# Weight differences moved from GpSimd to VectorE, norms by half rows, and last rows finished as two halves, in a one-core decoder block

## The chip, the cores and the metric

The kernel runs on one core of one Trainium2 chip. A core has TensorE (PE, matrix multiply), VectorE (DVE), ScalarE (ACT), GpSimd (POOL) and SyncE (SP, which here only issues DMAs); DMA engines move data between device memory and the on-chip SBUF, and TensorE writes to PSUM banks. The metric is the device time of one execution in microseconds (us); less is better. Line numbers, as L1287, are lines of the kernel before.

## The reference

One decoder block on a residual stream of 1024 tokens by 1024 columns, all in float32: RMS norm, 8 heads of forgetting attention and 8 heads of stick-breaking attention, an output projection onto the residual; RMS norm and cross-attention over 256 memory tokens (4 heads); RMS norm and a gated feed-forward with a causal convolution of width 3 over 2 x 2816 columns; a last RMS norm. Cut to the parts that the change touches:

```python
o = jnp.einsum('bhqk,bhkd->bhqd', p.astype(v.dtype), v)
x = x + jnp.einsum('bsc,cd->bsd', _merge(o), w_o)      # memory output, onto the residual
h = _rmsnorm(x, ffn_norm_g[l])                         # feed-forward norm
u = jnp.einsum('bsd,df->bsf', h, w_up[l])
...
x = x + jnp.einsum('bsf,fd->bsd', jax.nn.silu(gate) * val, w_down[l])
return _rmsnorm(x, final_norm_g)                       # last norm
```

`_rmsnorm` multiplies each row by the inverse root of the mean of its squares plus 1e-6, and by a gain.

## The kernel before

**Float32 as pairs.** A float32 operand is split into a high part (rounded by ScalarE or GpSimd) and a low part (the rest, subtracted by VectorE); `mm3` (L208 to L210) makes a product of three matmuls, high by high, high by low and low by high. So each operand costs a rounding and a subtraction, and TensorE waits for the later of the two.

**Fast products.** The memory output, the up product and the down product use a seven-product scheme for 2 x 2 blocks: sums and differences of operand blocks are formed first, and the products are added to several outputs. The residual x lies in eight tiles of 128 rows, `xr[0]` to `xr[7]`, each of two half rows of 512 columns (`lo_`, `hi_`).

**The planned stretch.** From the memory values to the first two of 22 up blocks the order is not written out but planned: `on(engine, length, function, after, take, give, at, ...)` adds a step with an assumed length, the steps it follows, the buffers it takes and gives, and a due time `at`, and `Plan.run` lays the steps out by simulating the engines. Among the steps that are ready on an engine the one with the smallest `at` goes first, and none starts more than 12 (`AHEAD`) before its `at`. What comes out is an order for each engine's queue; the times are forgotten. On the chip each queue is then worked off strictly in that order, so that a step that waits holds up all behind it. SyncE's queue (loads and spills) and GpSimd's (sums, splits, small powers, and the DMAs that add to their destination) are ordered this way too.

**Steps around the change, in order of their due times.** `values_steps` makes the memory values of the second half of the tokens; `mo_steps(k, ...)` makes product 7, 5, 3, 6 and 4 of the memory output (`o7`, `o5`, `o3`, `o6`, `o4`), each of four steps f of two splits (ACT high, L1308, DVE low, L1311) and four matmul groups of three. `outs` adds the banks of a product to `xr` or to a helper (`u`, L1344); `accumulate` adds a helper to `xr[4 + j]` by a DMA that GpSimd issues (L1144). The weight differences `t2s` (b11 = b22 - b11, VectorE) and `t4s` (b21 = b21 - b11, GpSimd), both at L1287, feed o6 and o4:

```python
t2s = [on(DVE, LOW, tt(V, b11[f], b22[f], b11[f], sub), [split_steps[5, 1][f]], at=58 + f, lock=True) for f in range(4)]
t4s = [on(POOL, SUM, tt(G, b21[f], b21[f], b11[f], sub), [loads[6 + f // 2], t2s[f]], at=66 + f, lock=True)
       for f in range(4)]
```

`finals[row]` collects what must be done before a row of x is complete. `norm_steps(0, 78)` and `norm_steps(1, 85)` then make the feed-forward norm of rows 0 to 3 and 4 to 7: a square of the whole row with its sum (ACT, L1427), mean (DVE, L1430), inverse root as a power (POOL, L1434), scaling into a tile `xn` (DVE, L1437), and a spill of the row to device memory (`spills`, SP). `tr` transposes the four scaled rows on TensorE (L1450), and the transposes are split into operands `b` (L1467, L1471) and, in the second half, `t1` and `t2` with sums formed by DMAs onto `f` (`onto_f1`). There are seven `xn` buffers. `gate_steps` and `sum_steps` make the weight operands of the first up blocks: four sums on GpSimd for each (L1611) and splits (L1595 to L1600). The up products read all of these.

**The loop and the end.** The 20 other up blocks run in a plain loop, then the down product (`dn_product`) in seven passes of eleven steps. The last passes complete rows 4 to 7 and rows 0 to 3: `finish` adds the bank to the low half of the row (L1956), squares both halves (L1961), adds the two sums (L1962), takes mean and power (L172, L174), multiplies the whole row by the root and the gain (L1964), and stores it (L1965).

Of the kernel before, what the change touches and what calls it, by code (L numbers as in the profile page):

```python
# [10 lines left out]
F32 = mybir.dt.float32  # L11
# [125 lines left out]
def hybrid_block(ctx, tc, x, mem, w, wf, pcol, bfg, fing, out):  # L137
# [1194 lines left out]
    finals = {j: [] for j in range(TB)}  # L1332
# [23 lines left out]
    for j in range(4):  # L1356
        def copy(j=j):
            A.activation(a22n12[j], o5[j], AF.Copy)

        c_ = on(ACT, ROUND, copy, [split_steps[5, "out"][j]] + [accs["s4x", i] for i in range(2)], at=outs_at)  # L1360
        outs(5, j, "STPS"[j], ([j], add_to(xr[j][:, hi_], o5, j)), after=[c_])
        finals[4 + j].append(accumulate(("p5", j), xr[4 + j][:, hi_], a22n12[j], [c_], 58))
# [6 lines left out]
    t4s = [on(POOL, SUM, tt(G, b21[f], b21[f], b11[f], sub), [loads[6 + f // 2], t2s[f]], at=66 + f, lock=True)  # L1369
# [4 lines left out]
    for j in range(4):  # L1374
        outs(3, j, "PSPS"[j], ([j], add_to(xr[j][:, hi_], o3, j, sub, True)))
# [3 lines left out]
    for j in range(4):  # L1379
        l_ = outs(6, j, "PSPS"[j], ([j], add_to(xr[j][:, hi_], o6, j)), ([], add_to(u[j], o6, j)), after=[u7[j]])  # L1380
        for c in (hi_, lo_):
            finals[4 + j].append(accumulate(("v", j, c.start), xr[4 + j][:, c], u[j], l_, 76))
# [32 lines left out]

    ssr = [[small.tile([P, 4], F32, tag=g, bufs=2, name=g) for g in ("ss", "rs")] for _ in range(2)]
    xns, spills = {}, {}

    def norm_steps(th, at):
        out_ = []  # L1420
        ss, rs = ssr[th]
        for j in range(4):
            row = 4 * th + j

            def square(j=j, row=row):
                xns[th, j] = wk.tile([P, D], F32, tag="xn", name="xn")
# [27 lines left out]
    norm0 = norm_steps(0, 78)  # L1454
# [180 lines left out]
    sum_steps(0, g0, v0, 86, {"m": [tmps], "s1": free, "s2": free, "s3": free, "a22": free, "s4": []}, {"s4": ["xn"]})  # L1635


    norm1 = norm_steps(1, 85)
    t_steps = {}

    def rest(i):

        if "rest" not in tiles:
            t = [qkp["f"].tile([P, 1024], F32R, tag=g, name=f"bt_{g}", bufs=b) for g, b in
                 (("q", 2), ("q", 2), ("k1", 2), ("k1", 2), ("k20", 1))]
            t = sum([views(t_, 2) for t_ in t], [])
            for n in range(3):
                t += views(vp.tile([P, 2, 1024], F32R, tag="v", name=f"bt_v{n}").rearrange("p k c -> p (k c)"), 4)
            tiles["rest"] = t
        return tiles["rest"][i]  # L1650
# [42 lines left out]
    for k in range(4):  # L1693
# [14 lines left out]
        x_ = last_turn = on(PE, 436, turn, norm1, ["T"], ["xn"] * 4 * (k == 3), at=86 + k)  # L1708
# [167 lines left out]
    def dn_product(fa, fb, held=0, done=None):  # L1876
# [10 lines left out]
        for f in range(H):  # L1887
# [169 lines left out]
```

## Time and profile before

| | us |
|---|---|
| median of 3 runs (lowest, highest) | 1600.13 (1599.53, 1602.65) |
| profiled execution, its own time | 1604.29 |
| span from first to last instruction in it | 1602.2 |
| busy in the span: PE, DVE, ACT | 1529.2, 1214.4, 783.8 |
| busy in the span: POOL | 533.3 |
| granted TensorE clock, share of full speed | 0.989 |

TensorE is busy for 95% of the span, so its idle stretches are what can be won; an average over the span does not say where they are. Busy time of an engine counts an instruction from its start to its end, also where it is held up inside.

### The profile page before, as it was taken

To read this page: it belongs to the slowest core of one execution; us is meant where nothing else is said; L and a number is where in the kernel's file an instruction comes from. 1 tells how busy PE (TensorE), PEld (TensorE's weight loads), DVE (VectorE), ACT (ScalarE), POOL (GpSimd) and SP (SyncE) were. 2 spreads that over 40 slices of the span, in tenths; PEclk is the share of its full clock that TensorE was granted. 3 is DMA by queue.
4 is the path that set the end of the run, shared out by engine and by line. 5 is a ranking of instruction groups with operands and counts; after the bars stand their busy time and mean duration, and the time that the engine had idled before them with its cause. 6 is when DMAs were issued, how large, how long until landed. Compare 5 with 4: busy or idle time off the path is not lost.

```text
span 1602.2 us, 22089 instructions
## 1 busy us (share of the span) xinstructions
PE 1529.2 (95%) x7684; PEld 1270.6 (79%) x7684; DVE 1214.4 (76%) x2070; ACT 783.8 (49%) x1534; POOL 533.3 (33%) x652
## 2 busy tenths in 40 slices
PE   7999999999999888999999889999999999999997
PEld 7677887887898766878887767878888888788886
DVE  7378777877877774365439988999999999786565
ACT  7368768757867551043325463333333333444443
POOL 3032323432432210123222445544445442233331
PEclk9999999999999999999999999999999999999998
DMA  5211021111115557312146454222222223998782
GB/s 178 95 66 66 27 64 60 37 54 66 40 54 184 193 164 247 122 53 78 42 141 161 92 145 139 76 83 93 86 85 79 79 82 107 325 291 198 146 180 105
DMA packets 78223, 183.54 MB, mean 115 GB/s; under 512 B 8728, under 2 KB 8856, under 8 KB 77856
## 3 DMA queue, kind: packets, MB, share of 16 engines
q1 hardware_dynamic: 62976, 152.63, 27.6%
q0 software_dynamic: 14688, 29.37, 10.3%
q8 instruction: 60, 0.98, 0.3%
q14 instruction: 51, 0.42, 0.1%
q10 hardware_dynamic: 448, 0.14, 0.0%
HBM read 130.69 MB, written 33.59 MB: 103 GB/s over the span
## 4 chain that ended last, share of the span: by engine, by line
PE 61%; DVE 17%; issue 8%; ACT 6%; DMA 5%; POOL 2%; SPq 0%; POOLq 0%; DVEq 0%; ACTq 0%
PE up_p L208 4%; PE up_p L209 4%; PE up_p L210 4%; PE dn L209 4%; PE dn L210 4%; PE dn L208 4%; PE pt L746 3%; PE pq L208 2%; PE pq L209 2%; PE pq L210 2%; PE po L763 2%; PE pqm L210 2%; PE pqm L209 2%; PE pqm L208 2%; PE po L762 2%
## 5 line engine op out<-in xcount | busy, mean ns | idle before, releaser
L703 POOL TENSOR_TENSOR p<-p,aw 128x383 f32<-128x383 f32 (+4 forms) x64 | 79.7, 1245 | 175.4 <-DVE aw L697 144.6
L209 PE MATMUL dn<-opb,opa 128*128 128x512 f32 x308 | 120.8, 392 | 2.7 <-DVE opb L1529 2.7
L754 DVE TENSOR_TENSOR ptl<-pt,pth 128x512 fp32r<-128x512 f32 x192 | 103.5, 548 | 25.2 <-ACT pth L750 23.7
L750 ACT ACTIVATE pth<-pt 128x512 fp32r<-128x512 f32 x192 | 92.7, 490 | 61.1 <-PE pt L746 55.2
L210 PE MATMUL dn<-opb,opa 128*128 128x512 f32 x308 | 120.8, 392 | 0.0
L208 PE MATMUL dn<-opb,opa 128*128 128x512 f32 x308 | 118.7, 390 | 0.7 <-ACT opb L1526 0.7
L746 PE MATMUL pt<-zid,p 128*128 128x128 f32 x576 | 95.3, 274 | 4.7 <-DVE ptl L754 4.5
L746 PEld LDWEIGHTS pt<-zid,p 128*128 128x128 f32 x576 | 72.4, 141 | 23.8 <-DVE ptl L754 6.9
L1540 POOL TENSOR_TENSOR tmp<-wv 128x512 f32<-128x512 f32 x20 | 33.4, 1672 | 166.0 <-DMA wv<-in_w_dram 156.1
L412 DVE TENSOR_TENSOR wlo<-wraw,whi 128x512 fp32r<-128x512 f32 x84 | 69.4, 854 | 20.7 <-ACT whi L407 20.3
L763 PE MATMUL po<-ptl,v 128*128 128x512 f32 x192 | 69.0, 359 | 9.6 <-DVE ptl L754 9.4
L1770 ACT ACTIVATE yv<-cv,cw 128x1024 f32<-128x1024 f32 x22 | 27.4, 1243 | 99.3 <-DVE cv L1802 98.7
L194 POOL TENSOR_SCALAR whi<-wraw 128x512 fp32r<-128x512 f32 x48 | 30.2, 643 | 134.7 <-issue 51.7
L680 POOL TENSOR_SCALAR p<-p,fx 128x128 f32<-128x128 f32 (+3 forms) x64 | 49.0, 768 | 74.9 <-DVE fx L620 64.2
L209 PE MATMUL up_p<-b,a 128*128 128x512 f32 x176 | 68.7, 390 | 1.9 <-DVE b L1471 1.9
L209 PEld LDWEIGHTS dn<-opb,opa 128*128 128x128 f32 x308 | 58.3, 189 | 15.2 <-DVE opb L1529 3.1
L208 PE MATMUL up_p<-b,a 128*128 128x512 f32 x176 | 68.8, 391 | 1.0 <-ACT b L1467 1.0
L762 PE MATMUL po<-pth,v 128*128 128x512 f32 x192 | 68.6, 357 | 0.7 <-ACT pth L750 0.6
L210 PE MATMUL up_p<-b,a 128*128 128x512 f32 x176 | 68.5, 389 | 0.0
L208 PEld LDWEIGHTS dn<-opb,opa 128*128 128x128 f32 x308 | 57.9, 188 | 13.2 <-ACT opb L1526 1.1
L210 PEld LDWEIGHTS dn<-opb,opa 128*128 128x128 f32 x308 | 58.3, 189 | 12.3
L407 ACT ACTIVATE whi<-wraw 128x512 fp32r<-128x512 f32 x84 | 50.0, 626 | 30.9 <-DMA wraw<-in_w_dram 16.1
(502 smaller groups left out, 5225.7 us busy)
## 6 DMA issues: line engine op xcount, KB each, us to landing
wraw<-in_w_dram SPq DMA_DIRECT2D x136, 256.0 KB, 3.0
a_d<-yv SPq DMA_DIRECT2D x22, 512.0 KB, 2.6
wg<-in_w_dram SPq DMA_DIRECT2D x20, 512.0 KB, 3.4
wv<-in_w_dram SPq DMA_DIRECT2D x20, 512.0 KB, 3.5
dn<-a_d POOLq DMA_DIRECT2D x32, 256.0 KB, 7.1
dn<-a_d SPq DMA_DIRECT2D x24, 256.0 KB, 8.7
dn<-in_w_dram SPq DMA_DIRECT2D x24, 256.0 KB, 7.8
xr<-mos POOLq DMA_DIRECT2D x20, 256.0 KB, 5.5
```

The source lines that it names most:

```text
L208: T.matmul(o, lt[0], rt[0], start=start, stop=False)
L209: T.matmul(o, lt[0], rt[1], start=False, stop=False)
L210: T.matmul(o, lt[1], rt[0], start=False, stop=stop)
L407: A.activation(t["hi"][:, c], t["raw", n], AF.Copy)
L412: in_turn("low", lambda: V.tensor_tensor(t["lo"][:, c], t["raw", n], t["hi"][:, c].bitcast(F32), op=ALU.subtract))
L680: G.tensor_scalar(out=c_["p"], in0=c_["p"], scalar1=c_["fx"][:, 4:5], scalar2=0.0, op0=ALU.mult, op1=ALU.add)
L703: G.tensor_tensor(c_["p"][:, :n0 - 1], c_["p"][:, :n0 - 1], c_["a"][:, 1:], op=ALU.mult)
L746: T.transpose(pt[:, j * P:(j + 1) * P], self.rows[j]["p"][:, kb * P:(kb + 1) * P], ident)
L750: A.activation(t[:, 512 - n:], self.sp["pt", kb][:, 512 - n:], AF.Copy)
L754: V.tensor_tensor(t[:, 512 - n:], self.sp["pt", kb][:, 512 - n:], self.sp["th", kb][:, 512 - n:].bitcast(F32), op=ALU.subtract)
L762: T.matmul(self.po[:, c], lv, self.sp["th", kb][:, c], start=kb == 0, stop=False)
L763: T.matmul(self.po[:, c], lv, self.sp["tl", kb][:, c], start=False, stop=kb == 4 * self.g + 3)
```

## The change

Seven edits, in the order of the diff:

1. `finals` is kept for each half row; the halves of a row become complete separately.
2. The four differences `t4s` go from GpSimd to VectorE, due at 58 + f in place of 66 + f. The DMAs that add `u` to rows 4 to 7 are due at 74 in place of 76.
3. The feed-forward norm squares a row as two half rows, each once its half is complete, into the weight tile `b22` as scratch, with the factor 1/1024 inside the square; the mean is one instruction that adds the two sums and the epsilon. The norm of rows 0 to 3 is due at 70 in place of 78 (and its low-half squares 8 earlier than that step's others), that of rows 4 to 7 at 85.5 in place of 85.
4. The scaled rows 6 and 7 lie in a tile of another pool (`xnv` in `vp`); the first half's norm takes its `xn` buffer at the scaling and not at the square.
5. `sum_steps` of the first up block is due at 95 in place of 86.
6. The tiles that the second half's operands lie in are allocated one by one at first use.
7. In `finish` the high half of each row, complete before the last product, is squared and multiplied by the gain (on GpSimd) ahead, in `half_done`; after the product the low half alone is added, squared and multiplied by root and gain (VectorE) while ScalarE multiplies the high half by the root. `half_done` of the last four rows is called before the last matmuls of the last pass.

The diff, cut where lines only move or repeat:

```diff
-    finals = {j: [] for j in range(TB)}
+    finals = {(j, c): [] for j in range(TB) for c in range(2)}
...
-    t4s = [on(POOL, SUM, tt(G, b21[f], b21[f], b11[f], sub), [loads[6 + f // 2], t2s[f]], at=66 + f, lock=True)
+    t4s = [on(DVE, LOW, tt(V, b21[f], b21[f], b11[f], sub), [loads[6 + f // 2], t2s[f]], at=58 + f, lock=True)
            for f in range(4)]
...
-        for c in (hi_, lo_):
-            finals[4 + j].append(accumulate(("v", j, c.start), xr[4 + j][:, c], u[j], l_, 76))
+        for n, c in ((1, hi_), (0, lo_)):
+            finals[4 + j, n].append(accumulate(("v", j, c.start), xr[4 + j][:, c], u[j], l_, 74))
...
+    free_b22 = split_steps[3, 1] + t2s
+
+    def xn_tile(th, j):
+
+        if th and j > 1:
+            return lazy("xv", lambda: vp.tile([P, 2, D], F32, tag="v", name="xnv"))[:, j - 2, :]
+        return wk.tile([P, D], F32, tag="xn", name="xn")
...
-            def square(j=j, row=row):
-                xns[th, j] = wk.tile([P, D], F32, tag="xn", name="xn")
-                A.activation(xns[th, j], xr[row], AF.Square, accum_out=ss[:, j:j + 1])
+            def square(c, j=j, row=row):
+                A.activation(b22[j], xr[row][:, (lo_, hi_)[c]], AF.Square, scale=D ** -0.5, accum_out=(ss, rs)[c][:, j:j + 1])
 
             def mean(j=j):
-                V.tensor_scalar(out=rs[:, j:j + 1], in0=ss[:, j:j + 1], scalar1=1.0 / D, scalar2=EPS,
-                                op0=ALU.mult, op1=ALU.add)
+                V.tensor_scalar(out=ss[:, j:j + 1], in0=ss[:, j:j + 1], scalar1=rs[:, j:j + 1], scalar2=EPS,
+                                op0=add, op1=add)
...
             def scale(j=j, row=row):
+                xns[th, j] = xn_tile(th, j)
                 V.tensor_scalar(out=xns[th, j], in0=xr[row], scalar1=rs[:, j:j + 1], scalar2=None, op0=ALU.mult)
 
-            q_ = on(ACT, 1060, square, finals[row], ["xn"], at=at + j)
-            q_ = on(DVE, 150, mean, [q_], at=at + j)
+            e_ = 1 - th
+            sq = [on(ACT, ROUND + 200, lambda c=c, f=square: f(c), finals[row, c] + free_b22, at=at + j + ((-10, -2), (-2, -2))[th][c])
+                  for c in (th, 1 - th)]
+            q_ = on(DVE, 150, mean, sq, at=at + j + -2.5)
             q_ = on(POOL, 550, power, [q_], at=at + j - 3)
-            out_.append(on(DVE, 760, scale, [q_], at=at + j))
+            out_.append(on(DVE, 760, scale, [q_], ["xn"] * (not th or j < 2), at=at + j))
...
-    norm0 = norm_steps(0, 78)
+    norm0 = norm_steps(0, 70)
...
-    sum_steps(0, g0, v0, 86, {"m": [tmps], "s1": free, "s2": free, "s3": free, "a22": free, "s4": []}, {"s4": ["xn"]})
+    sum_steps(0, g0, v0, 95.0, {"m": [tmps], "s1": free, "s2": free, "s3": free, "a22": free, "s4": []}, {"s4": ["xn"]})
-    norm1 = norm_steps(1, 85)
+    norm1 = norm_steps(1, 85.5)
...
-        x_ = last_turn = on(PE, 436, turn, norm1, ["T"], ["xn"] * 4 * (k == 3), at=86 + k)
+        x_ = last_turn = on(PE, 436, turn, norm1, ["T"], ["xn"] * 2 * (k == 3), at=86 + k)
...
+    def half_done(tb, scratch):
+
+        t = rows[tb]
+        with tc.issue_after(last_round[0]):
+            A.activation(scratch, t[:, hi_], AF.Square, scale=D ** -0.5, accum_out=rsg[0][:, tb:tb + 1])
+        G.tensor_tensor(t[:, hi_], t[:, hi_], gb[:, hi_], op=ALU.mult)
+
     def finish(tb, o, scratch, op):
-        t = rows[tb]
+        t, (s0, s1) = rows[tb], [r_[:, tb:tb + 1] for r_ in rsg]
         V.tensor_tensor(t[:, lo_], t[:, lo_], o, op=op)
-        ss = small.tile([P, 4], F32, tag="ss", bufs=2, name="ssf")
-        rs = small.tile([P, 4], F32, tag="rs", bufs=2, name="rsf")
         with tc.issue_after(last_round[0]):
-            for i, c in enumerate((hi_, lo_)):
-                A.activation(scratch[i], t[:, c], AF.Square, accum_out=ss[:, i:i + 1])
-        V.tensor_scalar(out=ss[:, 0:1], in0=ss[:, 0:1], scalar1=ss[:, 1:2], scalar2=None, op0=add)
-        rsqrt_mean(rs, ss, 1, D)
-        V.scalar_tensor_tensor(out=t, in0=t, scalar=rs[:, 0:1], in1=gb, op0=ALU.mult, op1=ALU.mult)
+            A.activation(scratch, t[:, lo_], AF.Square, scale=D ** -0.5, accum_out=s1)
+        V.tensor_scalar(out=s0, in0=s0, scalar1=s1, scalar2=EPS, op0=add, op1=add)
+        G.tensor_tensor(s1, s0, mhalf[:, :1], op=ALU.pow)
+        V.scalar_tensor_tensor(out=t[:, lo_], in0=t[:, lo_], scalar=s1, in1=gb[:, lo_], op0=ALU.mult, op1=ALU.mult)
+        A.activation(t[:, hi_], t[:, hi_], AF.Identity, scale=s1)
         nc.sync.dma_start(out[tb * P:(tb + 1) * P, :], t)
...
-        finish(4 + j, o[j], (r7[j], r5[j]), add)
+        half_done(4 + j, r5[j])
+        finish(4 + j, o[j], r7[j], add)
...
-               lambda j, bank: finish(j, bank, (r1[j], ru[j]), sub))
+               lambda j, bank: finish(j, bank, r1[j], sub), lambda: [half_done(j, ru[j]) for j in range(4)])
```

## Rows read from the trace of the kernel before

**Rows 1.** Busy time by stretch: stretch, its length, PE, PEld, DVE, ACT, POOL, clock, DMA.

```profile
900.00:1000.00 100.00, 90.17 (x394) 70.22 (x395) 88.13 (x126) 49.20 (x81) 48.87 (x48) 0.97 0.47 125
...
1100.00:1200.00 100.00, 100.00 (x439) 82.06 (x439) 95.70 (x106) 34.50 (x44) 46.59 (x35) 1.00 0.26 90
...
1500.00:1603.00 103.00, 91.90 (x406) 75.77 (x404) 64.21 (x107) 43.65 (x91) 31.50 (x36) 0.96 0.62 154
```

**Rows 2.** TensorE's waits, 890 to 1000: waiter, releaser, us in total, times, longest.

```profile
PE mo L209 <- DVE mob L1311: 4.3, 1, 4.3
PE up_p L208 <- ACT s L1595: 2.0, 1, 2.0
PE up_p L209 <- DVE b L1471: 1.9, 2, 1.6
PE ptn L1450 <- DVE xn L1437: 1.4, 2, 0.7
PE ptn L1450 <- DVE bt_k L1705: 1.2, 2, 0.7
PE up_p L208 <- ACT b L1467: 1.0, 1, 1.0
```

**Rows 3.** Busy time by stretches of 10 us, columns as in the first group.

```profile
900.00:910.00 10.00, 9.44 (x34) 7.63 (x35) 10.00 (x15) 2.31 (x4) 3.32 (x3) 0.83 0.40 73
...
960.00:970.00 10.00, 7.43 (x27) 5.03 (x27) 7.34 (x13) 4.52 (x8) 4.24 (x5) 0.96 1.02 211
970.00:980.00 10.00, 10.00 (x40) 8.02 (x39) 9.35 (x11) 4.00 (x7) 7.11 (x6) 0.87 0.67 211
```

**Rows 4.** Timeline of VectorE: start, us, line, operation, count, idle time before.

```profile
886.62 1.28 DVE L1287 TENSOR_TENSOR mow<-mow,mow 128x512 f32<-128x512 f32 x2
890.56 0.69 DVE L1311 TENSOR_TENSOR moa<-mos,moa 128x512 fp32r<-128x512 f32 x1 [2.65 <-ACT moa L1308]
...
893.36 7.14 DVE L1311 TENSOR_TENSOR mob<-mow,mob 128x512 fp32r<-128x512 f32 x1
...
913.84 1.58 DVE L1311 TENSOR_TENSOR mob<-mow,mob 128x512 fp32r<-128x512 f32 x1 [0.34 <-ACT mob L1308]
...
922.90 0.67 DVE L1311 TENSOR_TENSOR mob<-mow,mob 128x512 fp32r<-128x512 f32 x1
```

**Rows 5.** Timeline of GpSimd.

```profile
892.72 4.08 POOL L1287 TENSOR_TENSOR mow<-mow,mow 128x512 f32<-128x512 f32 x3
896.46 3.86 POOL L1144 DMA_DIRECT2D xr<-mos  x4
...
913.58 1.29 POOL L1611 TENSOR_TENSOR tmp<-raw_g,tmp 128x512 f32<-128x512 f32 x1 [10.26 <-DVE ops L1600]
...
919.69 5.36 POOL L1144 DMA_DIRECT2D xr<-mos  x6 [2.10 <-DVE mos L1344]
```

**Rows 6.** The norm's tiles: count, shortest/median/longest ns, first and last start.

```profile
L1434 POOL TENSOR_TENSOR rs<-rs,cst x8: 550/1506/3241, 923.2 to 947.9; 128x1 f32<-128x1 f32 x8
...
L1427 ACT ACTIVATE xn<-xr x8: 1052/1061/1070, 918.8 to 946.5; 128x1024 f32<-128x1024 f32 x8
```

**Rows 7.** The chain that ended last, 940 to 976: start, us, what.

```profile
959.48 8.52 DMA f<-t2f
```

**Rows 8.** Timeline of the end: VectorE, ScalarE, GpSimd.

```profile
1592.08 0.68 DVE L1956 TENSOR_TENSOR dn_k<-dn_k,dn 128x512 f32<-128x512 f32 x1
...
1594.50 1.28 DVE L1964 SCALAR_TENSOR_TENSOR dn_k<-dn_k,rsf,dnv 128x1024 f32<-128x1024 f32 x1 [0.44 <-POOL rsf L174]
1595.70 0.21 DVE L1962 TENSOR_SCALAR ssf<-ssf 128x1 f32<-128x1 f32 x1
...
1596.83 1.28 DVE L1964 SCALAR_TENSOR_TENSOR dn_k<-dn_k,rsf,dnv 128x1024 f32<-128x1024 f32 x1 [0.73 <-POOL rsf L174]
...
1592.79 0.63 ACT L1961 ACTIVATE res_ptl<-dn_k 128x512 f32<-128x512 f32 x1
...
1592.96 1.50 POOL L174 TENSOR_TENSOR rsf<-rsf,cst 128x1 f32<-128x1 f32 x1 [0.23 <-DVE rsf L172]
```

More of the change, by code (lines that the diff above doesn't have):

```diff
@@ L1360, in hybrid_block @@
         c_ = on(ACT, ROUND, copy, [split_steps[5, "out"][j]] + [accs["s4x", i] for i in range(2)], at=outs_at)
-        outs(5, j, "STPS"[j], ([j], add_to(xr[j][:, hi_], o5, j)), after=[c_])
-        finals[4 + j].append(accumulate(("p5", j), xr[4 + j][:, hi_], a22n12[j], [c_], 58))
+        outs(5, j, "STPS"[j], ([(j, 1)], add_to(xr[j][:, hi_], o5, j)), after=[c_])
+        finals[4 + j, 1].append(accumulate(("p5", j), xr[4 + j][:, hi_], a22n12[j], [c_], 58))
     for a in range(2):
@@ L1386, in hybrid_block @@
     for j in range(4):
-        outs(4, j, "PSPS"[j], ([4 + j], add_to(xr[4 + j][:, lo_], o4, j)))
-        finals[j] += [accs["u", j], accs["ul", j]]
+        outs(4, j, "PSPS"[j], ([(4 + j, 0)], add_to(xr[4 + j][:, lo_], o4, j)))
+        finals[j, 1].append(accs["u", j])
+        finals[j, 0].append(accs["ul", j])
     ti = to + 8
@@ L1423, in norm_steps @@
             row = 4 * th + j
-            def square(j=j, row=row):
-                xns[th, j] = wk.tile([P, D], F32, tag="xn", name="xn")
-                A.activation(xns[th, j], xr[row], AF.Square, accum_out=ss[:, j:j + 1])
+            def square(c, j=j, row=row):
+                A.activation(b22[j], xr[row][:, (lo_, hi_)[c]], AF.Square, scale=D ** -0.5, accum_out=(ss, rs)[c][:, j:j + 1])
             def mean(j=j):
-                V.tensor_scalar(out=rs[:, j:j + 1], in0=ss[:, j:j + 1], scalar1=1.0 / D, scalar2=EPS,
-                                op0=ALU.mult, op1=ALU.add)
+                V.tensor_scalar(out=ss[:, j:j + 1], in0=ss[:, j:j + 1], scalar1=rs[:, j:j + 1], scalar2=EPS,
+                                op0=add, op1=add)
             def power(j=j):
-                G.tensor_tensor(rs[:, j:j + 1], rs[:, j:j + 1], mhalf[:, :1], op=ALU.pow)
+                G.tensor_tensor(rs[:, j:j + 1], ss[:, j:j + 1], mhalf[:, :1], op=ALU.pow)
             def scale(j=j, row=row):
+                xns[th, j] = xn_tile(th, j)
                 V.tensor_scalar(out=xns[th, j], in0=xr[row], scalar1=rs[:, j:j + 1], scalar2=None, op0=ALU.mult)
-            q_ = on(ACT, 1060, square, finals[row], ["xn"], at=at + j)
-            q_ = on(DVE, 150, mean, [q_], at=at + j)
+            e_ = 1 - th
+            sq = [on(ACT, ROUND + 200, lambda c=c, f=square: f(c), finals[row, c] + free_b22, at=at + j + ((-10, -2), (-2, -2))[th][c])
+                  for c in (th, 1 - th)]
+            q_ = on(DVE, 150, mean, sq, at=at + j + -2.5)
             q_ = on(POOL, 550, power, [q_], at=at + j - 3)
-            out_.append(on(DVE, 760, scale, [q_], at=at + j))
+            out_.append(on(DVE, 760, scale, [q_], ["xn"] * (not th or j < 2), at=at + j))
             spills[row] = on(DMA, 100, lambda row=row: nc.sync.dma_start(x2_d[row * P:(row + 1) * P, :], xr[row]),
-                             finals[row], at=at + j, late=3500)
+                             finals[row, 0] + finals[row, 1], at=at + j, late=3500)
         return out_
@@ L1634, in hybrid_block @@
     free = split_steps[6, 1] + t4s
-    sum_steps(0, g0, v0, 86, {"m": [tmps], "s1": free, "s2": free, "s3": free, "a22": free, "s4": []}, {"s4": ["xn"]})
-    norm1 = norm_steps(1, 85)
+    sum_steps(0, g0, v0, 95.0, {"m": [tmps], "s1": free, "s2": free, "s3": free, "a22": free, "s4": []}, {"s4": ["xn"]})
+    norm1 = norm_steps(1, 85.5)
     t_steps = {}
     def rest(i):
[L1643 to L1650, printed above, removed]
+        if i < 10:
+            g, b = (("q", 2), ("q", 2), ("k1", 2), ("k1", 2), ("k20", 1))[i // 2]
+            return lazy(("rest", i // 2), lambda: views(qkp["f"].tile([P, 1024], F32R, tag=g, name=f"bt_{g}", bufs=b), 2))[i % 2]
+        n = (i - 10) // 4
+        return lazy(("restv", n), lambda: views(vp.tile([P, 2, 1024], F32R, tag="v", name=f"bt_v{n}")
+                                                .rearrange("p k c -> p (k c)"), 4))[(i - 10) % 4]
     def t_view(q, i):
@@ L1874, in op_tile, with dn_product @@
         return pairs(pool.tile([P, 1024], F32R, tag=tag, name=f"op{nm}"))
-    def dn_product(fa, fb, held=0, done=None):
+    def dn_product(fa, fb, held=0, done=None, ready=None):
         nonlocal step
@@ L1896, in dn_product @@
                 kept.append((f, oa, ob))
+        if ready is not None:
+            ready()
         for j in range(4):
```

4 lines of the change are left out of this document (2 added, 2 removed).

## The prediction

> **What bounds the kernel now.** I read the share of busy time first, then the span cut into stretches of 100 us, to find where TensorE is idle. In the loop it is full, and VectorE with 95.70 of 100 us nearly so [rows 1]. The change touches the planned stretch, whose end lies in 900 to 1000, and the tail. In the former TensorE is busy 90.17 of 100 us at a granted clock of 0.97, with VectorE at 88.13: TensorE starves while VectorE looks full.
>
> The view of waits says on what it starves [rows 2]. The largest is one wait of 4.3 us for one low part of o3 (L1311). Then 4.3 us in sum around the first half's transposes (1.4 for the scaled rows, 1.9 and 1.0 for `b`), and 3.2 us later (2.0 for a split of a weight sum, 1.2 for banks of the second half's transposes).
>
> The timelines say why. VectorE's low part at 893.36 took 7.14 us, where the two differences in front of it took 1.28 us together, so about 0.6 us each [rows 4]. In that time GpSimd ran three of the four `t4s` sums (4.08 us) and issued four DMAs (3.86 us) [rows 5]. An instruction that counts as busy was held up for 6.5 us. Behind the idle time the granted clock of 900 to 910 is 0.83 [rows 3], a mix of the 2.4 and the 1.2 GHz level: 1.7 us of full-speed work lost. The same views show 0.96 and 0.87 in 960 to 980 [rows 3], another 0.4 and 1.3 us.
>
> **The change part by part**, as time on TensorE's path, against the profiled execution's 1604.29 us.
>
> *The four differences.* On VectorE they are four instructions of the kind of L1287, 4 x 0.6 = 2.4 us [rows 4]. They become ready with `t2s`, whose last two start at 886.62; behind those VectorE idles 2.65 us until 890.56 [rows 4]. That gap covers them, so I cost them at nothing; without it they cost 2.4 us in front of o3's last split. GpSimd loses what held the low part. With some 0.6 us in place of 7.14 it would end near 894, before TensorE runs dry at 896.2 (the low part's end at 900.5 less the 4.3 us wait). Gain 4.3 us, and 1.7 us of clock behind it: **-6.0**. What is late next there is nothing that I can see: o6's splits follow with the slack that VectorE gets back.
>
> Could the four DMA issues have held VectorE, and not the sums? They stay, and would keep 3.9 of the 7.1 us, so that the wait shrinks to some 0.7 us even so: -3.6 and part of the clock. Against it, at 922.90 a low part of the same form took 0.67 us while GpSimd issued six DMAs in a row [rows 4, 5]. I take the sums.
>
> *The first half's norm.* In the kernel before, o6's outputs are followed by squares of 1.06 us, then powers that stand behind six DMA issues of 5.36 us on GpSimd, and last 1.5 us in the median and 3.24 at the longest, against 0.55 for a free one [rows 5, 6]. Now the low halves are squared long before, the last square is a half (0.63 us by its kin in the tail [rows 8]), and with a due time of 67 to 70 against 74 the powers go ahead of the DMAs where they are ready. I estimate that the scaled rows come 5 us earlier against o6's end (0.4 from the square, 4 to 5 from the issues). TensorE has o4 to do meanwhile, so transposes and their splits slip in between. The waits for scaled rows (1.4) and the longer of those for `b` (1.6) go; what is left of `b` is the pace of the splits: **-3.0**, between 0 and -4.3.
>
> *The second half's norm.* Its four squares run until 946.5 [rows 6], since each takes an `xn` buffer that the first half frees late; now two buffers do, and the other two rows have a tile of their own. From the last transposes hang `t2`, the DMA onto `f` of 8.52 us [rows 7], the load of the second block's weights, and so the waits of 2.0 and 1.2 us and the clock of 960 to 980. Some of this hides under the products of the first up blocks, some waits for VectorE all the same. I take half of 3.2 + 1.7: **-2.5**, between 0 and -4.9.
>
> *The sums of the first up block*, due 9 later, go from beside o6 and o4 to beside the norm's scalings and splits. A sum of 1.29 us at 913.58 stood beside a low part of 1.58 us [rows 4, 5]: 0.9 us more than 0.67. Four sums hold up VectorE for 0 to 3.6 us where it now matters more: **+1.8**. The Trainium skill has a rule that speaks against this edit (page "SBUF — State Buffer", section "Who interferes with whom"): a VectorE instruction with two SBUF inputs and a GpSimd instruction that reads SBUF exclude each other for the whole of the one that started first. The 1.58 us agree; by the rule each moved sum takes its blocking along, and the sum below would be 1.8 us worse.
>
> *Separate halves, lazy tiles, the mean in one instruction, DMAs at 74:* no instruction more on TensorE; two half squares are 0.2 us longer than a whole one on ScalarE (2 x 0.63 against 1.06 [rows 6, 8]), which is busy 49.20 of 100 us here [rows 1]. Nothing; if ScalarE were full, 8 x 0.2 = 1.6 us. The spills, due 8 earlier, still wait for complete rows on SyncE, with only weight loads behind them.
>
> *The tail.* The last row goes from its add at 1592.08 to the end of its last multiply at 1598.11: 6.03 us [rows 8]. On the way its sum (1595.70) waits behind the whole multiply of the row before (1.28 us), and that row's power lasted 1.50 us. New path: add 0.68, half square 0.63 and the read of its sum 0.2 (an estimate, as the 0.21 of the small sum), mean 0.21, power 0.55, half multiply 0.68 beside ScalarE's half; 2.95 us, and hops of 0.05 to 0.1 us each, some 0.4 (an estimate from the gaps between these rows). 6.03 - 3.35 = **-2.7**, between -0.6 (only the shorter multiply, 1.28 - 0.68) and -3.1. The eight new GpSimd multiplies (about 1.3 us each, as the sum at 913.58) run beside splits of passes in which VectorE is busy 64.21 of 103 us [rows 1]; that slack covers them. If they stood in front of the last power, they would cost 1.3 us.
>
> Sum: -6.0 - 3.0 - 2.5 + 1.8 - 2.7 = -12.4 us; 1604.29 - 12.4 = 1591.9 for a profiled execution. The median of the runs is 4.16 us below the profiled one; off it the same sum gives 1600.13 - 12.4 = **1587.7 us**.
>
> **The rivals.**
>
> *A. The norm gains nothing, the sums carry their blocking along.* VectorE is the true bound of 900 to 1000 [rows 1], and only the first stall and the tail pay: -6.0 + 3.6 - 2.7 = -5.1, 1595.0 us. For it: 88.13 us busy. Against it: 6.5 us of those are one held instruction. The Trainium skill's rule above would lead here.
>
> *B. All waits go.* -6.0 - 4.3 - 4.9 - 3.1 = -18.3, 1581.8 us. For it: TensorE has o4 and the first up products to fill with. Against it: VectorE must do the same work, plus 2.4 us, in less time.
>
> *C. Slower: the norm's small steps block VectorE's queue.* With due times of 67 to 70 means and scalings stand ahead of o4's splits (73 and later) in an in-order queue, and each row's chain of half square, mean, power and hops, 0.63 + 0.21 + p + 0.4 us, could be waited out by VectorE with TensorE starved of o4's operands. The norm's gain is then void (-9.4 is left) and four rows cost 4 x (1.24 + p). At p = 0.55 that is +7.2, 1597.9 us; at the median p = 1.5 it is +11.0, 1601.7 us; at the longest, 3.24, it is +17.9, 1608.6 us [rows 6]. It is slower by over 0.2% from p of about 1.9 us. For it: the powers' lengths before. Against it: those stood among DMA issues and sums, and four rows overlap.
>
> *D. The differences' move doesn't free VectorE*, because the DMA issues held it: the forecast less 2.4 to 4 us, inside its range.
>
> **How the numbers follow.** A measurement of this kernel can tell about 0.2%, 3.2 us, from no change. Forecast 0.50 (its own range 1583 to 1593), A 0.18 (of it 0.04 within 0.2%), B 0.13, C 0.19 (0.08 within 0.2%, 0.11 slower). Faster 0.50 + 0.14 + 0.13 = 0.77, the same 0.12, slower 0.11. The range goes from B's side with some room, 1579.5, to 1600.0, where A is in and most of C is out: about 0.05 below, 0.15 above.
>
> **What would show it.** No low part of L1311 above 2 us near 893, no wait of TensorE above 1 us there, and a clock of 1.00 behind it. `t4s` on VectorE right behind `t2s`. The first half's powers ahead of most of the DMAs onto rows 4 to 7, scaled rows before o4's last group. Row 7's last square well before 946.5, and the DMA onto `f` landed some 12 us earlier than 968. In the tail, some 3.3 us from the last add to the last multiply. The prediction is wrong if VectorE waits for a power for over 2 us with o4's splits behind it, if sums of GpSimd stretch the splits of the transposes, or if a new wait in 900 to 960 takes the place of the 4.3 us.

## The result, and the profile after

| us | before | after |
|---|---|---|
| median (lowest to highest) of 6 runs each | 1599.83 (1599.14 to 1603.84) | 1590.2 (1587.33 to 1595.71) |
| profiled execution | 1604.29 | 1587.33 |
| its span | 1602.2 | 1585.5 |

The ratio is 0.9938, 95% interval 0.9919 to 0.9957: 9.9 us faster, where 12.4 were forecast. The two profiled executions differ by 17.0 us, more than the medians do: the one before is slower than all six runs beside it, and the changed one is the fastest of its six. Of the 17.0 us, 3.9 lie ahead of the first matmul of o7 (868.40 before, 864.53 after), where no edit acts yet. So I read the profiles from that matmul to the start of the last silu of the loop (the "middle" below), and the tail by itself.

Busy times of the middle, of the kernel before and then of the changed one; columns as in [rows 1]:

```profile
868.40:1391.20 522.80, 505.03 (x2205) 409.18 (x2203) 481.58 (x573) 194.81 (x276) 239.16 (x197) 0.99 0.37 112
```

```profile
864.50:1376.00 511.50, 501.12 (x2205) 407.61 (x2203) 475.64 (x577) 195.76 (x291) 233.43 (x193) 1.00 0.38 113
```

The same 2205 matmuls take 11.3 us less: TensorE idles 10.4 us in place of 17.8, and its busy time for equal work is 3.9 us shorter, with a mean granted clock of 1.00 in place of 0.99.

Line numbers of the changed kernel are 8 to 11 higher from the norm on: L1434 is now L1442, L1437 is L1446, L1471 is L1482, L1595 and L1600 are L1606 and L1611, the sums L1611 are L1622, and L1795 (`cv`, an add that empties a bank of the up product) is L1804.

TensorE's waits in the changed kernel, 860 to 990, which answer to [rows 2]:

```profile
PE mo L209 <- DVE mob L1311: 2.5, 1, 2.5
PE ptn L1461 <- DVE xn L1446: 1.7, 1, 1.7
PE up_p L208 <- ACT s L1606: 1.2, 1, 1.2
PE mo L208 <- DVE xr L1344: 1.2, 1, 1.2
PE up_p L208 <- DVE cv L1804: 1.2, 1, 1.2
PE up_p L208 <- DVE bt_k L1714: 0.6, 1, 0.6
PE up_p L210 <- DVE s L1611: 0.6, 1, 0.6
```

The 4.3 us near 893 are gone, and so are the waits for `b`. There is again one wait for a low part of L1311, but another one: of o4, at 918. The 1.2 us for `xr`, at 900, is new too.

Its clock by stretches of 10 us, answering to [rows 3]:

```profile
900.00:910.00 10.00, 9.80 (x43) 8.12 (x44) 7.63 (x14) 3.30 (x7) 0.61 (x1) 1.00 0.01 2
910.00:920.00 10.00, 7.55 (x30) 5.88 (x29) 8.59 (x15) 4.21 (x12) 9.74 (x14) 0.89 1.06 295
920.00:930.00 10.00, 8.28 (x42) 6.12 (x41) 9.73 (x13) 6.48 (x14) 8.03 (x8) 0.94 0.85 212
...
970.00:980.00 10.00, 10.00 (x45) 8.11 (x45) 10.00 (x13) 4.69 (x6) 7.28 (x5) 1.00 0.00 0
```

The mix of the two levels (2.4 and 1.2 GHz) now stands in 910 to 930, behind TensorE's stops of 2.5 us (o4's low part) and 1.7 us (scaled rows), and not in 900 to 910 and 960 to 980.

The timelines of VectorE and GpSimd in the changed kernel, answering to [rows 4, 5]:

```profile
880.95 2.02 DVE L1287 TENSOR_TENSOR mow<-mow,mow 128x512 f32<-128x512 f32 x3
...
889.53 0.68 DVE L1311 TENSOR_TENSOR mob<-mow,mob 128x512 fp32r<-128x512 f32 x1
...
890.73 1.41 DVE L1287 TENSOR_TENSOR mow<-mow,mow 128x512 f32<-128x512 f32 x2
...
912.68 0.76 DVE L1446 TENSOR_SCALAR xn<-xr,rs 128x1024 f32<-128x1024 f32 x1
...
917.42 0.67 DVE L1311 TENSOR_TENSOR mob<-mow,mob 128x512 fp32r<-128x512 f32 x1
918.59 2.70 DVE L1611 TENSOR_TENSOR a<-raw_g,a 128x512 fp32r<-128x512 f32 x1 [0.50 <-POOL a L1608]
921.21 1.74 DVE L1446 TENSOR_SCALAR xn<-xr,rs 128x1024 f32<-128x1024 f32 x1
...
889.01 3.78 POOL L1144 DMA_DIRECT2D xr<-mos  x4
...
918.34 1.66 POOL L1442 TENSOR_TENSOR rs<-ss,cst 128x1 f32<-128x1 f32 x1
...
919.47 2.92 POOL L1622 TENSOR_TENSOR tmp<-raw_pth,raw_ptl 128x512 f32<-128x512 f32 x1
```

The low part that took 7.14 us takes 0.68, while the same four DMAs are issued beside it. The last row of the first half's norm has a power of 1.66 us, then its scaling stands behind a split of 2.70 us, beside which a moved sum runs. Two of the eight L1287 differences, at 890.73, stand behind the low part of 889.53 and not ahead of it.

The norm's tile `rs`, answering to [rows 6], and the DMA onto `f` in the chain that ended last, to [rows 7]:

```profile
L1442 POOL TENSOR_TENSOR rs<-ss,cst x8: 547/1130/1957, 911.4 to 936.4; 128x1 f32<-128x1 f32 x8
```

```profile
949.16 6.39 DMA f<-t2f
```

Powers are shorter (median 1.13 in place of 1.51 us) and the last starts at 936.4 in place of 947.9. The DMA lands at 955.6 in place of 968.0; 3.9 us of each difference lie ahead of the middle.

The end, answering to [rows 8]:

```profile
1576.66 0.75 DVE L1979 SCALAR_TENSOR_TENSOR dn_q<-dn_q,rsg,dnv 128x512 f32<-128x512 f32 x1 [0.44 <-POOL rsg L1978]
1577.33 0.20 DVE L1977 TENSOR_SCALAR rsg<-rsg,rsg 128x1 f32<-128x1 f32 x1
1577.45 0.68 DVE L1974 TENSOR_TENSOR dn_k<-dn_k,dn 128x512 f32<-128x512 f32 x1
...
1578.20 0.72 ACT L1980 ACTIVATE dn_k<-dn_k,rsg 128x512 f32<-128x512 f32 x1 [0.81 <-POOL rsg L1978]
1578.83 0.61 ACT L1976 ACTIVATE res<-dn_k 128x512 f32<-128x512 f32 x1
...
1580.44 0.75 DVE L1979 SCALAR_TENSOR_TENSOR dn_k<-dn_k,rsg,dnv 128x512 f32<-128x512 f32 x1 [0.66 <-POOL rsg L1978]
```

From the last row's add to the end of its last multiply there are 3.74 us in place of 6.03. But the add waits behind a multiply and a mean of rows before, and the square behind ScalarE's multiply of another row. From the last L208 matmul to the span's end there are 9.6 us in place of 11.2 (1575.91 to 1585.46; 1591.06 to 1602.24).

### The profile page after: what moved, and what is told of

It is laid out like the page before. It is cut to its first block, busy times and chain, and to the rows that moved or that the text cites. A ratio compares the mean times of both kernels' runs of the same rounds, so it can differ in the third digit from the quotient of the medians.

```text
span 1585.5 us, 22098 instructions
## 1 busy us (share of the span) xinstructions
PE 1523.2 (96%) x7684; PEld 1267.5 (80%) x7684; DVE 1206.8 (76%) x2066; ACT 789.8 (50%) x1558; POOL 534.9 (34%) x656
## 3 DMA queue, kind: packets, MB, share of 16 engines
q0 software_dynamic: 14688, 29.37, 10.4%
## 4 chain that ended last, share of the span: by engine, by line
PE 57%; DVE 19%; issue 8%; ACT 7%; DMA 6%; POOL 2%; SPq 0%; POOLq 0%; DVEq 0%; ACTq 0%
PE dn L209 4%; PE dn L210 4%; PE dn L208 4%; PE pt L746 3%; PE up_p L208 3%; PE up_p L209 3%; PE up_p L210 3%; PE pq L208 2%; PE pq L209 2%; PE pq L210 2%; PE po L763 2%; PE pqm L210 2%; DMA wraw<-in_w_dram 2%; PE pqm L209 2%; PE pqm L208 2%
## 5 line engine op out<-in xcount | busy, mean ns | idle before, releaser
L210 PE MATMUL dn<-opb,opa 128*128 128x512 f32 x308 | 120.6, 391 | 0.0
L208 PE MATMUL dn<-opb,opa 128*128 128x512 f32 x308 | 118.9, 391 | 0.0
L208 PE MATMUL up_p<-b,a 128*128 128x512 f32 x176 | 69.3, 394 | 0.0
L210 PE MATMUL up_p<-b,a 128*128 128x512 f32 x176 | 68.5, 389 | 0.0
L208 PEld LDWEIGHTS dn<-opb,opa 128*128 128x128 f32 x308 | 58.3, 189 | 12.3
L210 PEld LDWEIGHTS dn<-opb,opa 128*128 128x128 f32 x308 | 58.3, 189 | 12.2
```

The source lines that it names most:

```text
L208: T.matmul(o, lt[0], rt[0], start=start, stop=False)
L210: T.matmul(o, lt[1], rt[0], start=False, stop=stop)
```

## The experiments

Ratios are against runs of the kernel before on the same chip. The middle is from the profile of each.

| kernel | median, us | ratio [95%] | middle, us | idle in it | last L208 to end |
|---|---|---|---|---|---|
| before | | 1 | 522.8 | 17.8 | 11.2 |
| changed | 1590.2 | 0.9938 [0.9919, 0.9957] | 511.5 | 10.4 | 9.6 |
| differences alone | 1596.51 | 0.9966 [0.9953, 0.9979] | 517.2 | 13.4 | 11.2 |
| tail alone | 1598.77 | 0.9981 [0.9969, 0.9993] | 521.8 | 16.5 | 9.5 |
| norm and sums alone | 1594.11 | 0.9961 [0.9948, 0.9975] | 515.3 | 12.5 | 11.3 |
| all but the tail | 1590.46 | 0.9947 [0.9928, 0.9965] | 511.2 | 10.1 | 11.3 |
| changed, sums due 86 | 1590.35 | 0.9934 [0.9917, 0.9951] | 512.7 | 11.9 | 9.5 |
| changed, norm due 78 | 1593.48 | 0.9949 [0.9933, 0.9964] | 515.7 | 12.3 | 9.5 |
| changed, norm due 74 | 1593.78 | 0.9958 [0.9943, 0.9972] | 517.7 | 13.8 | 9.5 |
| changed, scalings later | 1595.59 | 0.9970 [0.9959, 0.9981] | 520.6 | 15.5 | 9.5 |
| changed, sums on VectorE | 1593.62 | 0.9960 [0.9945, 0.9974] | 517.1 | 15.4 | 9.5 |
| changed, multiplies behind | 1590.16 | 0.9930 [0.9918, 0.9943] | 513.6 | 11.0 | 9.7 |
| before, no differences | 1596.63 | 0.9970 [0.9958, 0.9982] | 515.3 | 12.3 | 11.2 |
| before, issues behind sums | 1599.74 | 0.9998 [0.9985, 1.0012] | 520.0 | 17.8 | 11.2 |

Three kernels have one and the same order in the middle, that of the changed one: 511.5, 511.2 and 513.6. So one profile's middle is known to some 2.4 us.

**The differences alone** (before, with this):

```diff
-    t4s = [on(POOL, SUM, ..., at=66 + f, lock=True)
+    t4s = [on(DVE, LOW, ..., at=58 + f, lock=True)
```

> The kernel before with one edit: the four differences t4s go to VectorE, due at 58 + f. TensorE's, ScalarE's and SyncE's queues keep their order. Theory (the sums held VectorE): no low part of L1311 above 2 us near 893, TensorE's wait of 4.3 us gone, the clock of 900 to 910 at 1.00, 4 to 6 us faster than the kernel before. Rival (the DMA issues held it, or the freed VectorE only runs into the next wait): a low part near 893 still takes 3 us or more, or TensorE gets back less than 2 us.

5.4 us (3.4 to 7.5) against the term of 6.0. The wait of 4.3 us is gone; the waits around the norm are those of [rows 2], but for a tenth or two.

**The tail alone** (before, with edit 7, in its core):

```diff
-        V.scalar_tensor_tensor(out=t, in0=t, scalar=rs[:, 0:1], in1=gb, ...)
+        V.scalar_tensor_tensor(out=t[:, lo_], in0=t[:, lo_], scalar=s1, in1=gb[:, lo_], ...)
+        A.activation(t[:, hi_], t[:, hi_], AF.Identity, scale=s1)
```

> The kernel before with the last edit alone: rows finished as two halves. Theory of the prediction: 2.7 us faster, from the last add to the last multiply some 3.3 us. Rival, from the trace of the changed kernel: 3.7 us from the last add to the last multiply, and the add itself later behind the multiply of a row before, because ScalarE's square of the last row stands behind the multiply of the row in front of it; so 1.5 us faster at most. The rest of the time as in the kernel before.

The interval allows 1.1 to 5.0 us. The stretch after the last L208 says it more closely: 1.7 us less here, and 9.5 to 9.7 in every kernel with the new tail against 11.2 to 11.3 in every one without.

**No differences at all** (before):

```diff
-    t4s = [on(POOL, SUM, tt(G, b21[f], b21[f], b11[f], sub), [loads[6 + f // 2], t2s[f]], at=66 + f, lock=True)
+    t4s = [on(DMA, 0, lambda: None, [loads[6 + f // 2], t2s[f]], at=58 + f)
```

> The kernel before with the four differences t4s left out altogether (o4's second operand is then the wrong one; GpSimd and VectorE do nothing in their place). If the four differences cost VectorE nothing where the change puts them, this gains what their move alone gained, about -5.4 us, 0.9966 of before. If their 2.4 us on VectorE are paid on the path, it gains 2 us or more beyond that, 0.995. If the DMA issues on GpSimd held the low part near 893, it is still held for over 3 us here, and the gain is at most 2 us.

Timeline of VectorE and GpSimd in it:

```profile
894.86 0.68 DVE L1311 TENSOR_TENSOR mob<-mow,mob 128x512 fp32r<-128x512 f32 x1
...
894.06 3.72 POOL L1144 DMA_DIRECT2D xr<-mos  x4
```

Its ratio is that of the differences alone within 0.0004: on VectorE they cost nothing that can be seen in the runs (the middles differ by 1.9 us, which is within their scatter). And four DMA issues by themselves don't hold the low part.

**Issues behind the sums** (before; only GpSimd's order differs: third and fourth difference, then the four DMAs):

```diff
-  finals[4 + j].append(accumulate(("p5", j), ..., [c_], 58))
+  finals[4 + j].append(accumulate(("p5", j), ..., [c_], 71))
```

> The kernel before with one change of order: GpSimd issues the four DMAs behind the fourth difference and not between the third and the fourth. If sums alone hold VectorE's low part near 893, it is let go when the fourth sum ends, some 5.4 us after the first began: about 4.8 us in place of 7.14, TensorE's wait 2 in place of 4.3, and 2 to 3 us less in all. If issues hold it too, it stays at 7 us or more, and so does the wait of 4.3.

The timelines of VectorE and GpSimd in it:

```profile
891.99 6.46 DVE L1311 TENSOR_TENSOR mob<-mow,mob 128x512 fp32r<-128x512 f32 x1
...
891.35 5.32 POOL L1287 TENSOR_TENSOR mow<-mow,mow 128x512 f32<-128x512 f32 x4
896.30 3.89 POOL L1144 DMA_DIRECT2D xr<-mos  x4
898.54 2.98 POOL L1611 TENSOR_TENSOR tmp<-raw_pth,raw_ptl 128x512 f32<-128x512 f32 x1
```

Neither expectation: the sums end at 896.67, the low part only at 898.45, 1.8 us into the DMA issues that follow the sums without a gap, when the next sum is about to start. The same issues alone hold nothing; whether they hold it here, or a sum whose record ends too soon, no run separates. TensorE's wait is 2.9 us and the clock of 900 to 910 is 1.00, yet the median moves by 0.6 us, within the interval: waits of 1.2 us for `s` and 1.0 us for `xr` are new, and TensorE's idle time in the middle is 17.8 us as before.

**Norm and sums alone** (the changed kernel with differences and tail as before) and **all but the tail** (the changed kernel with the tail as before):

```diff
-    t4s = [on(DVE, LOW, ..., at=58 + f, lock=True)
+    t4s = [on(POOL, SUM, ..., at=66 + f, lock=True)
...
-        half_done(4 + j, r5[j])
-        finish(4 + j, o[j], r7[j], add)
+        finish(4 + j, o[j], (r7[j], r5[j]), add)
```

The second has only the lower part of it.

> The changed kernel with the differences back on GpSimd (due at 66 + f) and the old end of the rows: the norm by half rows, the other tile, the later sums and the due times alone. By the prediction's terms (-3.0 - 2.5 + 1.8) some 3.7 us less than before, 0.9977 of it. If the edits simply add up, what the change gains beyond the differences alone and the tail alone is left, -1.5 us, 0.999. If the norm's earlier steps need the time that the differences' move frees on VectorE, nothing is gained or some us are lost, since the low part near 893 is held as before (a wait of 3 to 4 us for it).

> The changed kernel with the old end of the rows (whole squares and multiplies): edits 1 to 6, the tail left out. Alone, the differences gained 5.4 us and the norm with the sums 6.2 us. If these two add up, they give 11.6 us here, 0.9928 of before, more than the whole change gained. If both remove the same idle time, it is what the whole change gained (9.9 to 11 us) less the tail, 8 to 9 us, 0.9945 to 0.995. From the last high-by-high matmul to the end of the span there are 11.1 us as before, against 9.6 in the changed kernel.

Alone, the norm and the sums gain 6.2 us (4.0 to 8.3), more than their terms (3.7) and more than the 1.5 us that are left over. Together with the differences it is 8.5 us (5.6 to 11.5), where 5.4 and 6.2 add up to 11.6. The intervals don't exclude the sum; the middle says 7.5 us (norm and sums) and 5.6 (differences) against 11.6 together, so some 1.5 us overlap, less than the profiles scatter. The timelines of the norm and sums alone show that part of the first stall shrinks there without the move:

```profile
891.40 5.23 DVE L1311 TENSOR_TENSOR mob<-mow,mob 128x512 fp32r<-128x512 f32 x1
...
890.77 4.08 POOL L1287 TENSOR_TENSOR mow<-mow,mow 128x512 f32<-128x512 f32 x3
894.50 3.88 POOL L1144 DMA_DIRECT2D xr<-mos  x4
896.75 2.95 POOL L1287 TENSOR_TENSOR mow<-mow,mow 128x512 f32<-128x512 f32 x1
```

The low part is let go at 896.63, ahead of the fourth sum, and TensorE waits some 2.4 us for it in place of 4.3. So 1.9 us of the first stall go without the move, and the two gains overlap there.

**Due times put back** (changed kernel; one line each):

```diff
-    sum_steps(0, g0, v0, 95.0, ...)
+    sum_steps(0, g0, v0, 86, ...)
...
-    norm0 = norm_steps(0, 70)
+    norm0 = norm_steps(0, 78)
```

The third has 74 in place of 78.

> The changed kernel with the sums of the first up block due at 86 again. Theory (the moved sums carry their blocking along to where the first half's scalings and splits run): with the sums early, the held splits near 918 to 923 go and the waits around the transposes shrink by about 2 us, but low parts near 900 to 915 are held instead and o4's operands come later; within 2 us of the changed kernel either way. Rival (the move was what paid in the middle): slower than the changed kernel by 3 us or more.

> The changed kernel with the norm of rows 0 to 3 due at 78 again. Theory (the early due time puts scalings in front of o4's splits on VectorE, which costs the new wait of 2.5 us for an o4 operand and gains nothing): that wait goes, and the kernel is as fast as the changed one or up to 2.5 us faster. Rival (the early norm pays, by transposes that start sooner): 2 us slower or more, with scaled rows later against o4's end.

> The changed kernel with the norm of rows 0 to 3 due at 74, half way back. If the norm's due time only shifts TensorE's wait from o4's low part (2.5 us) to the scaled rows, the sum of these two stays near 4 us and the time within 2 us of the changed kernel. If there is a place between in which both are short, they fall below 2 us in sum, and the time is some 2 us below the changed kernel's. In 1000 to 1060 the two waits for cv (1.9 us in sum, as in the kernel before) come back if VectorE's order there does.

The sums' due time makes no difference that can be measured. At 86 the split that took 2.70 us beside a moved sum takes 1.13 (at 922.01), but VectorE is held early instead: 1.66 and 1.77 us near 894, and 1.09 us twice near 910. With the norm at 78 the wait for o4's low part is gone and that for scaled rows is 2.3 us; at 74 they are 1.9 and 2.6; at 70 they are 2.5 and 1.7. At 74 neither is short, and 70 is the best of the three by ratio and middle, though the intervals overlap.

**Scalings later** (changed kernel; squares, means and powers stay early):

```diff
-  out_.append(on(DVE, 760, scale, [q_], ..., at=at + j))
+  out_.append(on(DVE, 760, scale, [q_], ..., at=at + j + 11.5 * (not th)))
```

> The changed kernel with the scalings of rows 0 to 3 alone due 11.5 later, behind o4's last split, while squares, means and powers stay early. If scalings that stand ahead of o4's splits in VectorE's queue caused the wait of 2.5 us for one of o4's low parts, that wait falls below 0.5 us, and the wait for scaled rows grows from 1.7 us to 2 or 3: the time is that of the changed kernel within 1.5 us. If the wait came from something else (ScalarE's rounding, sums of GpSimd), it stays at 2 us or more, and the time is some 2 us worse.

The two longest of TensorE's waits in the middle, then VectorE's timeline around the longer:

```profile
PE up_p L208 <- DVE cv L1804: 6.0, 2, 5.4
...
PE up_p L209 <- DVE b L1482: 2.6, 1, 2.6
```

```profile
1007.74 1.75 DVE L1540 TENSOR_TENSOR ops<-wv,ops 128x512 fp32r<-128x512 f32 x1 [1.78 <-POOL ops L1539]
1009.41 1.75 DVE L1819 TENSOR_TENSOR yv<-yg,yv 128x512 f32<-128x512 f32 x1
1011.08 1.75 DVE L1820 SCALAR_TENSOR_TENSOR yv<-yg,yv 128x512 f32<-128x512 f32 x1
1012.75 0.68 DVE L1804 TENSOR_TENSOR cv<-up_p,cg 128x512 f32<-128x512 f32 x1
```

The wait for o4's low part is gone: the scalings in front of it were its cause. Still the kernel is some 5 us slower than the changed one. A wait for `b` returns, and 90 us later, in an up block, the add that TensorE needs (`cv`) stands behind a split that waits 1.78 us for GpSimd, and behind two instructions of 1.75 us that take 0.69 in the changed kernel.

**Sums on VectorE** (changed kernel, first up block):

```diff
+            if n == 0:
+                return [on(DVE, LOW, lambda: V.tensor_tensor(dst(), a(), b(), op=op), after, at=at, lock=True)]
             return [on(POOL, SUM, ...)]
```

> The changed kernel with the four sums of the first up block on VectorE too, not on GpSimd. In the changed kernel VectorE's instructions beside these sums (918 to 931) took 2.70, 1.74, 1.08 and 1.03 us where 0.68 to 0.76 is usual, 3.7 us more in all. If the moved sums carry that blocking along, as the prediction's +1.8 says, four sums of 0.6 us on VectorE cost 2.4 us and free 3.7: the wait of 1.7 for scaled rows falls below 1 us and the time is 1 to 2 us below the changed kernel's. If VectorE is the bound of this stretch, 2.4 us more work there make it 1 to 3 us slower than the changed kernel.

The split of 2.70 us takes 1.13 here too (at 923.60), and the wait for scaled rows falls to 1.0 us, but later ones grow: 2.6 for `s`, 1.3 for `bt_v`, and 4.0 for `cv` and `cg` after 1000. By the ratios it gains 3.5 us less than the changed kernel, on the side of the second expectation, though the intervals overlap; whether VectorE's extra work or its new order does it stays open.

**Multiplies behind** (changed kernel; last four rows):

```diff
+        with tc.issue_after(m_):    # m_, q_: mean and square of the next row
+            V.scalar_tensor_tensor(out=t[:, lo_], ...)
+        with tc.issue_after(q_):
+            A.activation(t[:, hi_], t[:, hi_], AF.Identity, scale=s1)
```

> The changed kernel with the last four rows' final multiplies put behind the next row's work: ScalarE squares the last row before it multiplies high halves of rows 1 and 2, and VectorE adds the last row before row 1's multiply and takes its mean before row 2's. If these places in the queues cost the tail what the prediction missed, the last add starts 0.5 us earlier against the last matmul, and from it to the end of the last multiply there are 3.1 us in place of 3.74: together -1.1 us. Rival: the freed operations only wait for the power instead, and the stretch stays at 3.6 us or more.

The end of its timeline:

```profile
1577.58 0.69 DVE L1974 TENSOR_TENSOR dn_k<-dn_k,dn 128x512 f32<-128x512 f32 x1
...
1579.19 0.74 DVE L1982 SCALAR_TENSOR_TENSOR dn_k<-dn_k,rsg,dnv 128x512 f32<-128x512 f32 x1
1579.35 0.99 POOL L1978 TENSOR_TENSOR rsg<-rsg,cst 128x1 f32<-128x1 f32 x1 [1.06 <-DVE rsg L1977]
...
1580.28 1.24 SPq L1985 DMA_DIRECT2D out_dram<-dn_k  x2
1580.38 0.75 DVE L1982 SCALAR_TENSOR_TENSOR dn_k<-dn_k,rsg,dnv 128x512 f32<-128x512 f32 x1 [0.44 <-POOL rsg L1978]
```

The add comes 0.7 us earlier after the last L208 (0.88 us in place of 1.54) and the stretch to the last multiply shrinks to 3.55 us, less than expected, since the power now runs beside a multiply and takes 0.99. But from there to the end there are 5.3 us in place of 4.3: the stores of the last two rows now follow each other closely and take 3.2 us to land in the median, not 2.6. Nothing is won.

## Why the forecast came near, and which of its steps failed

**The first stall** (-6.0) was right. The wait of 4.3 us and the clock behind it are gone, 5.4 us by the runs. That the differences cost nothing was right too, but the gap of 2.65 us did not cover all of them: the last two of the eight L1287 differences run at 890.73, behind o3's last low part and ahead of another idle stretch (1.41 us, until 894.15). Rival D fell: the issues alone hold nothing. That a hold can outlast the sums by 1.8 us, into the issues behind them, was not in the prediction; the kernel with the issues behind the sums shows it.

**The first half's norm** (-3.0) failed. By the waits alone, 4.3 us (1.4 for scaled rows, 2.9 for `b` in [rows 2]) became 5.4: 1.7 for scaled rows, 2.5 for o4's low part and 1.2 for a bank. Behind the stops, the granted clock of 0.89 and 0.94 in 910 to 930, which is 1.00 in the kernel before, costs another 1.7 us. The step that failed is "TensorE has o4 to do meanwhile, so transposes and their splits slip in between": means, scalings and adds stand in front of o4's split in VectorE's queue. With the scalings later, that wait is gone. It is rival C's mechanism at a price of 2.5 us, not the 7 to 18 worked out there, as four rows overlap; and a new wait in 900 to 960 was one of the prediction's own signs of being wrong, though this one is smaller than the 4.3 us. The estimate that scaled rows come 5 us earlier held for three of the four rows. In the kernel before, then in the changed one (whose scalings are shown above), the end of o6 and the scalings:

```profile
918.18 0.39 PE L210 MATMUL mo<-mob,moa 128*128 128x512 f32 x1
...
925.68 0.75 DVE L1437 TENSOR_SCALAR xn<-xr,rs 128x1024 f32<-128x1024 f32 x1 [1.38 <-POOL rs L1434]
...
928.08 2.84 DVE L1437 TENSOR_SCALAR xn<-xr,rs 128x1024 f32<-128x1024 f32 x3 [0.98 <-POOL rs L1434]
```

```profile
909.64 0.39 PE L210 MATMUL mo<-mob,moa 128*128 128x512 f32 x1
```

Behind o6's last matmul the first scaling starts after 2.7 us in place of 7.1, but the last one ends after 12.9 in place of 12.4: TensorE waits 1.7 us for that row. The third piece, 1.2 us, comes from an edit that I had costed at nothing: four low-half squares on ScalarE from 894.02 to 897.10 stand between high parts of o6, VectorE idles 1.00 us at 897.65 for one of these, o3's adds follow late, and TensorE waits for the bank. A busy share of 49.20 didn't show that. These placings are read from the traces (with multiplies behind, in the same order, the bank's wait is 0.5 us); only the wait of 2.5 us was also taken away by a run.

**The second half's norm** (-2.5) was near. Its waits (2.0 for `s`, 1.2 for `bt_k`, 0.6 for `t1f`) became 1.8 and 0.6: -1.4. The granted clock of 960 to 980, which had cost 1.7 us, is 1.00. Together that is -3.1; no run separates it. Counted from the start of the middle, the DMA onto `f` lands 8.5 us earlier.

**The moved sums** (+1.8) cost nothing that can be measured, 86 against 95. The blocking is there, but one sum makes nearly all of it: the split of 2.70 us and the scaling of 1.74 behind it take 1.13 and 0.75 in both kernels without that sum beside them. The splits of 1.08 and 1.03 us, which the expectation for the sums on VectorE counts in, stand beside roundings of GpSimd (L1608). The three other sums (926.91 to 930.82) run beside adds and splits with one input in PSUM, which take 0.68 to 0.74 us as usual, and one split of 0.82. The Trainium skill (page "SBUF — State Buffer", section "Who interferes with whom") makes a VectorE instruction with two SBUF inputs and a GpSimd instruction that reads SBUF exclude each other. The trace agrees for the splits of 2.70 and 0.82 us, which have two inputs in SBUF; by the records the sum starts 0.9 us after the longer one, so which came first can't be read there, and why the scaling, with one such input, is held too, no run shows. So a moved sum takes blocking along only where VectorE has such an instruction beside it, and at 86 these sums held VectorE about as long (1.66 and 1.77 us, and 1.09 twice).

**What the forecast did not have** lies after 1000. In the kernel before `cv` makes TensorE wait 2.6 us in three pieces, 1.9 of them between 1000 and 1060. In the changed kernel one of 1.2 us is left. VectorE's order differs there; first the differences alone, with the wait, then the changed kernel:

```profile
1027.37 1.11 DVE L1529 TENSOR_TENSOR s<-tmp,s 128x512 fp32r<-128x512 f32 x1 [1.85 <-ACT s L1526]
1028.40 0.68 DVE L1795 TENSOR_TENSOR cv<-up_p,cg 128x512 f32<-128x512 f32 x1
```

```profile
1021.18 0.69 DVE L1804 TENSOR_TENSOR cv<-up_p,cg 128x512 f32<-128x512 f32 x1
...
1023.12 1.23 DVE L1540 TENSOR_TENSOR s<-tmp,s 128x512 fp32r<-128x512 f32 x1 [1.25 <-ACT s L1537]
```

In the one a split that itself waits stands ahead of the add for `cv`, in the other behind it. With the sums at 86 or the norm at 78 the 1.9 us are back (0.4 with the norm at 74); with the norm there the kernel is slower in the median, with the sums it isn't. The norm and sums alone have the changed kernel's order here, and no wait between 1000 and 1060. So part of what the norm and the sums gained in the profiles came by an order of later blocks that none of the seven edits names, and how much of the total it makes is not settled.

**The tail** (-2.7) was sized too high: 1.6 us by the profile. The path from the add lost 2.3 us, but the add starts 0.5 us later after the last matmul (1.08 us after the last L210's start, 0.57 before), and the square 0.7 us late; both stand behind work of earlier rows that the prediction's sum left out.

**The sum**: in the profiles the middle gave 11.3 us and the tail 1.6, 12.9 against 12.4 forecast. The medians differ by 9.6, so the two profiles, of an execution above all six before and of the fastest after, show more than the change is worth. That the total came near is in part luck: by the runs the norm and sums gave 6.2 us for 3.7, although the first half's term failed, and this made up for part of what the differences (5.4 for 6.0), the tail (1.6 for 2.7) and the overlap of the first two fell short. Of the middle's 11.3 us TensorE's waits make 6.9 (from 16.2 to 9.3 in sum); the rest is shorter busy time at a higher clock and gaps below the view's resolution, which I can't assign to edits. Rival A's time is 5 us too slow and B's 8 us too fast.

## What to carry to other kernels

An instruction that lasts ten times its usual length is the first thing to look for in a "busy" engine: here moving four small sums from GpSimd to VectorE, one line, gained 5.4 us alone, about as much as all the norm's restructuring (6.2 alone, 8.5 with both). In an in-order queue an earlier due time only chooses who waits; cost a moved step by what then stands behind it on its own engine, and a half square on an engine at 49% can still delay the next product (1.2 us here, as read from the trace). And when a plan changes, compare the order of later blocks too, since waits of 2 to 5 us can come or go there.

## What was unexpected of the hardware

- A VectorE instruction with two SBUF operands, blocked by a GpSimd sum, is not let go between sums that follow each other closely, and by the records it stays held into the DMA issues behind them (1.8 us past the last sum in two kernels): 7.14, 6.46 and 5.23 us for one low part. The same four issues without sums leave it at 0.68.
- It goes the other way too: the power on one column takes 0.55 us when free and 0.99 beside a half multiply of VectorE with two SBUF operands (0.75), ending 0.4 us after it.
- Identical orders of instructions give middles of 511.2 to 513.6 us, and the wait for scaled rows in them is 1.7, 1.7 and 2.9 us, so a wait of 1 us in one profile is no evidence for a total.
